# A hybrid decoder trunk on eight cores: a finer wrapping weight ring, squares and rotary sums on GpSimd, group-norm scaling on ScalarE

## The chip, the cores and the metric

The kernel runs on all 8 cores of one Trainium2 chip, one batch element per core, in one launch. Cores 0 to 3 are one die, 4 to 7 the other. The metric is the device time of the slowest core, in microseconds (us).

Every kernel of this program has a second, slower state: in some executions the cores of one die (sometimes both) are granted a lower TensorE clock and the run takes up to 20% longer. Such runs are called slow and no difference here rests on them. Where a kernel had hardly any fast run, I quote its **undisturbed dies**: the median span of the four cores of a die whose clock was not lowered.

## The reference, cut to what matters

Four layers over 2048 tokens of width 1024; per layer a half-weighted SwiGLU, a token mixer with two groups of heads, and a second SwiGLU.

```python
h = x + 1/2 * SwiGLU_1(RMSNorm(x))            # d_ff = 2816
u = RMSNorm(h); aq|ak|av|rq|rk|rv|rg = u @ W_in
a = sliding_window_gqa(aq, ak, av, sinks)     # window 128
r = retention(rotary(rq), rotary(rk), rv)     # chunks of 128, 4 heads of 128
r = silu(rg) * GroupNorm(r)
h = h + concat([a, r]) @ W_out
x = h + 1/2 * SwiGLU_2(RMSNorm(h))
```

## The kernel before

Each core takes its sequence as four tiles of 512 tokens, two at a time. The two tiles X = 0 and X = 1 go through each stage with the same weights. A host-side list scheduler, run when the kernel is built, fixes the order on each engine. Its priority is the TensorE time that comes earlier in the same tile, and tile 1 is set back by a constant, so that tile 0's next stage fills tile 1's waits.

```python
RING = 24576                     # columns of bf16 weights held on chip
LAG = 22.0
def key():
    X = cur['X']
    return cur['p'][X] + (LAG if X else 0.0)
```

The weights stream through one ring. A unit is 4096 columns of gate/up weights (32 matmuls of 512 columns for each tile), 2816 of w_down, or 4096 of w_o (half of the output projection). A unit that does not fit before the end of the ring starts again at zero, and its load waits for every use of every unit that it overlaps.

```python
for n, x in enumerate(units):
    size = x.size
    if head + size > RING:
        head = 0                         # the rest of the ring stays empty
    gone = [y for y in live if y.off < b and a < y.off + y.size]
    ...
    for y in gone:
        o.war |= {q.i for q, _ in y.uses}    # all uses of the whole unit
```

The sum of squares of a norm is built while the stage before it writes its eight chunks: ScalarE squares a chunk, and TensorE adds it across partitions with a matrix of ones.

```python
def np_feed(k):
    q = VT('b')
    act(AF.Square, lambda: T(q)[:], lambda: hT[X][:, k, :], ...)
    mm(lambda e: e.matmul(T(v)[:], onesd[:], T(q)[:], start=(i == 0), stop=(i == KC - 1)), ...)
```

In the mixer VectorE does the rotary products and sums, and the end of the group norm with the gate:

```python
for i in range(2):                       # rotary: two products, then two sums of halves
    dve(... tensor_tensor(out=q[.. i ..], in0=rt[i, first half], in1=rt[i, second half], op=ALU.add))
...
for h in range(4):                       # (y - mean) * rstd, per head
    dve(... tensor_scalar(out=T(yn)[:, hs], in0=T(vy)[:, hs], scalar1=mean, scalar2=rstd,
                          op0=ALU.subtract, op1=ALU.mult))
dve(... tensor_tensor(out=T(ro)[:], in0=T(yn)[:], in1=gsl(blk), op=ALU.mult))
```

The softmax here doesn't subtract the row's maximum and nothing guards it: scores larger than these inputs give would overflow.

## Time and profile before

| before | |
|---|---|
| all first runs, median (range) | 5324.35 us (5024.16 to 5688.27) |
| fast runs of all rounds | 5022 to 5036 us, with one of 5052 |
| profiled run, per core | 5001.8 to 5023.3 us, clock 0.989 to 0.991 |
| TensorE busy, idle | 4829.3, 194.0 us |
| VectorE, ScalarE, GpSimd busy | 37, 28, 6% |
| DMA packets | 64,543 for 362.92 MB |

The median of the first three runs mixes the two states; the fast runs have a mean of some 5,028 us.

In the profile, `L573` is line 573; PE, DVE, ACT and POOL are TensorE, VectorE, ScalarE and GpSimd; an entry after `<-` in brackets is what ended an idle stretch. TensorE's list of waits: line waited on, what released it, then us in all, times, and the longest. L539 is the ones-matmul of a norm, L573 the gate/up projection.

```profile
PE ps L539 <- ACT b L468: 36.2, 17, 7.1
PE ps L573 <- DVE nT L550: 29.1, 14, 4.7
PE ps L573 <- DMA ring<-w_gu: 9.8, 7, 2.5
```

The direct wait for weights is short. The two lines above it are the latency chain of a norm: square, ones-matmul, scale.

Second, GpSimd's timeline before one mixer's end (start, duration, then what ended the wait before it). These are the loads of the next gate/up units:

```profile
956.90 0.53 POOL L905 DMA_DIRECT2D ring<-w_gu  x1 [1.00 <-PE ps L609]
978.63 0.59 POOL L905 DMA_DIRECT2D ring<-w_gu  x1 [14.42 <-PE ps L609]
986.80 0.53 POOL L905 DMA_DIRECT2D ring<-w_gu  x1 [7.57 <-PE ps L740]
```

Three units, then none until the pair at 1057.68 that the prediction quotes. I quoted that pair, and did not count the three. The 42.90 us in its line are also not the whole pause: they count from GpSimd's last small copy (1014.10), while no load was issued for 70.9 us, from 986.80 on. At the eight seams, the places where a mixer hands over to the next gate/up stage, this pause was 51 to 71 us, always after three units.

One small VectorE operation with two on-chip inputs (duration min/median/max in ns):

```profile
L715 DVE TENSOR_TENSOR st<-st,epst x64: 145/155/275, 304.5 to 4750.6; 128x4 f32<-128x4 f32 x64
```

### The profile page before, as it was taken

The page shows a single profiled execution, that of the slowest core. Times are in us where ns is not written, and L with a number is a line of the kernel's source. Part 1 is how long each engine was busy: PE and PEld are TensorE (multiplying, and loading weights), DVE is VectorE, ACT ScalarE, POOL GpSimd, SP SyncE. Part 2 cuts the span into 40 slices and gives each one's busy share as a digit, 9 for nine tenths or more (in the row PEclk, how much of TensorE's full clock was granted, in tenths as well). Part 3 has the DMA queues.
Part 4 walks back from the last instruction along what each step waited for, and adds up shares of the span by engine and source line. Part 5 has one row for each costly group of instructions (what it writes and reads, how often), then busy time and mean ns, then how long its engine had stood idle before and what let it go on. Part 6 is the DMA issues. An engine that isn't in the chain of part 4 may idle for free.

```text
span 5023.3 us, 66149 instructions; the slowest of 8 cores (5001.8 to 5023.3 us)
## 1 busy us (share of the span) xinstructions
PE 4829.3 (96%) x23328; PEld 2235.8 (45%) x23800; DVE 1837.4 (37%) x3760; ACT 1413.1 (28%) x2346; POOL 277.2 (6%) x507
## 2 busy tenths in 40 slices
PE   8999999989999999999989999999999999999999
PEld 3444444434444444444434444444444444444444
DVE  2174122741227312173121741228322282222822
ACT  2144121441214412144121441214311153111521
POOL 1000000000000000000000000000000000000000
PEclk9999999999999999999999999999999999999999
DMA  6433344333443234433454333433334333344233
GB/s 128 77 67 54 71 75 78 64 52 71 75 79 65 52 71 78 78 65 65 72 127 71 71 66 71 79 72 64 63 68 82 68 62 68 72 74 75 54 73 74
DMA packets 64543, 362.92 MB, mean 72 GB/s; under 512 B 7904, under 2 KB 8160, under 8 KB 34656
## 3 DMA queue, kind: packets, MB, share of 16 engines
q0 software_dynamic: 53424, 339.76, 38.0%
q1 hardware_dynamic: 10800, 18.90, 1.3%
q8 instruction: 201, 3.29, 0.3%
q14 instruction: 118, 0.97, 0.1%
HBM read 689.98 MB, written 8.39 MB: 139 GB/s over the span
## 4 chain that ended last, share of the span: by engine, by line
PE 89%; ACT 3%; issue 3%; DVE 2%; DMA 2%; SPq 0%; DVEq 0%; POOL 0%; ACTq 0%; POOLq 0%
PE ps L573 46%; PE ps L584 24%; PE ps L609 8%; PE ps L830 4%; PE ps L740 2%; PE ps L539 2%; DMA ring<-w_gu 1%; ACT f L468 1%; ACT L468 1%; PE ps L647 1%; ACT b L468 1%; DMA hT<-xT 1%; PE ps L746 1%; PE ps L754 1%; PE ps L805 0%
## 5 line engine op out<-in xcount | busy, mean ns | idle before, releaser
L573 PE MATMUL ps<-nT,ring 128*128 128x512 bf16 x11027 | 2795.9, 382 | 58.7 <-DVE nT L550 29.1
L573 PEld LDWEIGHTS ps<-nT,ring 128*128 128x128 bf16 x11264 | 1105.6, 98 | 1397.8 <-issue 97.1
L584 PE MATMUL ps<-reg,ring 128*128 128x512 bf16 x5531 | 1651.4, 380 | 6.4
L577 DVE TENSOR_TENSOR reg<-ps,f 128x512 bf16<-128x512 f32 x704 | 477.5, 690 | 1954.9 <-PE ps L573 1777.3
L468 ACT ACTIVATE f<-ps 128x512 f32<-128x512 f32 (+1 forms) x884 | 515.9, 595 | 1927.7 <-PE ps L573 1867.7
L584 PEld LDWEIGHTS ps<-reg,ring 128*128 128x128 bf16 x5632 | 551.5, 98 | 661.6 <-issue 3.3
L609 PE MATMUL ps<-ring,nT 128*128 128x512 bf16 x1992 | 596.0, 379 | 10.2 <-ACT reg L468 2.7
L468 ACT ACTIVATE b<-hT 128x512 bf16<-128x512 f32 x416 | 258.6, 628 | 1031.3 <-DVE hT L586 868.3
L586 DVE SCALAR_TENSOR_TENSOR hT<-ps,hT 128x512 f32<-128x512 f32 x256 | 175.7, 690 | 805.3 <-PE ps L584 782.3
L468 ACT ACT_TABLE_LOAD x173 | 222.0, 1283 | 260.1 <-PE ps L573 139.4
L609 PEld LDWEIGHTS ps<-ring,nT 128*128 128x128 bf16 x2048 | 195.3, 98 | 218.4 <-issue 20.5
L550 DVE SCALAR_TENSOR_TENSOR nT<-hT,cn,f 128x512 bf16<-128x512 f32 x384 | 262.6, 748 | 60.5 <-ACT f L468 57.5
L830 PE MATMUL ps<-reg,ring 128*128 128x512 bf16 x996 | 251.8, 385 | 11.4 <-DVE reg L812 9.9
L905 POOL DMA_DIRECT2D ring<-w_gu x179 | 95.8, 536 | 2321.9 <-PE ps L573 1277.3
L468 ACT ACTIVATE b<-ps 128x512 bf16<-128x512 f32 (+1 forms) x312 | 175.6, 601 | 76.6 <-PE ps L647 59.4
L634 DVE TENSOR_TENSOR rt<-ps,rot 128x512 f32<-128x512 f32 x256 | 174.6, 682 | 61.1 <-PE ps L609 55.5
L539 PE MATMUL ps<-b,onesd 128*128 128x512 bf16 x402 | 154.4, 385 | 36.8 <-ACT b L468 36.2
L468 ACT ACTIVATE reg<-ps 128x512 f32<-128x512 f32 (+2 forms) x192 | 110.6, 598 | 200.5 <-PE ps L647 118.8
L830 PEld LDWEIGHTS ps<-reg,ring 128*128 128x128 bf16 x1024 | 99.0, 99 | 122.8 <-issue 19.9
L740 PE MATMUL ps<-nT,ring 128*128 128x512 bf16 x490 | 141.9, 379 | 2.2 <-DVE reg L728 0.9
L905 POOL DMA_DIRECT2D ring<-w_d x128 | 67.5, 530 | 1265.4 <-PE ps L573 1167.7
L832 DVE TENSOR_TENSOR hT<-ps,hT 128x512 f32<-128x512 f32 x128 | 87.1, 683 | 86.3 <-PE ps L830 83.4
(75 smaller groups left out, 1879.7 us busy)
## 6 DMA issues: line engine op xcount, KB each, us to landing
ring<-w_gu POOLq DMA_DIRECT2D x175, 1024.0 KB, 8.4
ring<-w_d POOLq DMA_DIRECT2D x128, 704.0 KB, 6.8
ring<-w_r POOLq DMA_DIRECT2D x32, 1024.0 KB, 8.9
ring<-w_o POOLq DMA_DIRECT2D x16, 1024.0 KB, 8.1
hT<-xT SPq DMA_DIRECT2D x32, 256.0 KB, 7.4
ring<-w_aq POOLq DMA_DIRECT2D x8, 1024.0 KB, 8.8
yT<-reg SPq DMA_DIRECT2D x32, 256.0 KB, 4.8
ring<-w_akv POOLq DMA_DIRECT2D x8, 512.0 KB, 5.1
```

The costliest lines, as they stand in the source:

```text
L468: return A('act', lambda e: e.activation(out=out(), in_=in_(), func=func, **{k: (v() if callable(v) else v) for k, v in kw.items()}), read ...
L539: mm(lambda e: e.matmul(T(v)[:], onesd[:], T(q)[:], start=(i == 0), stop=(i == KC - 1)), [q, 'onesd'], [v])
L550: dve(lambda e, k=k: e.scalar_tensor_tensor(out=dst(k), in0=hT[X][:, k, :], scalar=cn[:, cbase + k:cbase + k + 1], in1=T(r)[:], op0=ALU.mu ...
L573: mm(lambda e, v=v, a=a, k=k, x=x: e.matmul(T(v)[:], W(x, a, 128), nT[X][:, k, :], start=(k == 0), stop=(k == KC - 1)), [('n', X, k)], [v] ...
L577: dve(lambda e, sg=sg, pu=pu, fc=fc: e.tensor_tensor(out=reg[X][:, fc, :], in0=T(pu)[:], in1=T(sg)[:], op=ALU.mult), [pu, sg], rk(X, fc))
L584: mm(lambda e, v=v, fc=fc, x=x: e.matmul(T(v)[:], W(x, fc * 128, 128), reg[X][:, fc, :], start=(fc == 0), stop=(fc == FC - 1)), rk(X, fc), ...
L586: dve(lambda e, v=v, dc=dc: e.scalar_tensor_tensor(out=hT[X][:, dc, :], in0=T(v)[:], scalar=0.5, in1=hT[X][:, dc, :], op0=ALU.mult, op1=AL ...
L609: mm(lambda e, k=k: e.matmul(T(v)[:], nT[X][:, k, blk * 128:(blk + 1) * 128], W(x, k * 512, 512), start=(k == 0), stop=(k == KC - 1)), [(' ...
L634: dve(lambda e, i=i, off=off: e.tensor_tensor(out=rt[:, i, :].rearrange("p (h e) -> p h e", h=4), in0=X4(), in1=rot[:, g + off:g + off + 1 ...
L740: mm(lambda e, k=k, j=j, v=v: e.matmul(T(v)[:], W(xa, (k * 4 + j) * 128, 128), nT[X][:, k, :], start=(k == 0), stop=(k == KC - 1)), [('n', ...
L830: mm(lambda e, v=v, a=a, src=src, x=x, cc=cc: e.matmul(T(v)[:], W(x, a, 128), R_[:, src, :], start=(cc == 0), stop=(cc == 7)), rk(X, src), ...
L905: o = rec.add('pool', lambda e, x=x, j=j, w=w: e.dma_start(out=ring_t[:, x.off + j * w:x.off + (j + 1) * w], in_=x.src[:, j * w:(j + 1) * w]),
```

## The change

The intent is to take work from TensorE (squares) and from VectorE (rotary sums, group norm), to lay both on nearly idle engines, and to let weights arrive earlier. The core of the diff; `...` marks cuts. Two edits are not shown: 16 semaphores instead of 12 for the weight loads, and GpSimd operations that now wait for the one before.

```diff
-LAG = 22.0
+LAG = 23.0
+RESERVE = {'ps': 0, 'f': 1, 'b': 2, 'st': 1}     # buffers the scheduler keeps back
...
-            if eng == 'pool':
-                writes = list(writes) + ['poolq']      # GpSimd in program order
...
+            x.step = 2048 if x.size % 2048 == 0 else x.size // 2
...
-        def np_start():
+        def np_start(direct=False):
...
+            if acc is not None and i == 0:
+                act(AF.Square, lambda: T(acc)[:], lambda: hT[X][:, k, :], [('h', X, k)], [acc])
+                return
+            if acc is not None and i < KC - 2:
+                out = acc if i < KC - 3 else VT('b')
+                A('pool', lambda e: e.tensor_tensor(out=T(out)[:], in0=T(acc)[:], in1=T(q)[:], op=ALU.add), ...)
...
-                for i in range(2):
-                    dve(... tensor_tensor(... op=ALU.add), [('rt', i)], [q], 0.42)
+                A('pool', lambda e: e.tensor_tensor(out=T(q)[:]..., in0=half(0), in1=half(1), op=ALU.add), ...)
...
-                    dve(... tensor_scalar(... op0=ALU.subtract, op1=ALU.mult), [vy, st], [yn], 0.3)
+                    act(AF.Identity, T(yn)[:, hs], T(vy)[:, hs], ..., scale=rstd, bias=-mean*rstd)
-                dve(... tensor_tensor(out=T(ro)[:], in0=T(yn)[:], in1=gsl(blk), op=ALU.mult), ...)
+                A('pool', ... same operation ...)
...
-            if head + size > RING:
-                head = 0
+                q.a, q.b = a, min(a + x.step - a % x.step, a + RING - head)
+                head = (head + w) % RING
...
+                while live and live[0].off < q.off + w and q.off < live[0].off + live[0].b - live[0].a:
+                    o.war |= {z.i for z in live.popleft().uses}
```

## The prediction

> **What bounds the kernel now.** I read the cores first: 5001.8 to 5023.3 us, both dies alike, clock 0.99, a fast run. (The quoted median, 5324 us, mixes states; the lowest, 5024 us, is the fast one. I predict the fast state and compare with 5023.) The engine totals:
>
> ```profile
> PE 4829.3 (96%) x23328; PEld 2235.8 (45%) x23800; DVE 1837.4 (37%) x3760; ACT 1413.1 (28%) x2346; POOL 277.2 (6%) x507
> ```
>
> TensorE looks full, but matmul records overlap, so I count work. The chain of waits in order of time and the timeline of TensorE give its two rates:
>
> ```profile
> 93.86 10.74 PE ps L573 x49
> ...
> 1006.36 1.06 PE L754 MATMUL ps<-ring,nT 128*128 128x128 bf16 x16
> ```
>
> One 512-column matmul lasts 0.38 us, so 49 in 10.74 us is (10.74-0.38)/48 = 0.2158 us each; the 128-column ones take (1.06-0.22)/15 = 0.056. The code issues 21,528 of the first kind (1,344 for each of 16 tile-layers, 32 for the first norms, less 8 for the first block) and 2,272 of the second: 4,646 + 127 = **4,773 us** that no schedule removes. The other 250 us are 194 us of recorded idle time and about 55 us of lost clock (mean 0.989, 1.1% of the span). By windows of 25 us, the idle time lies at the start (21), the end (13), the turn to the second pair of tiles (17 at 2500-2550), six ends of FFN stages (21), and the eight mixer stages (103); 20 us are scattered. Here is a mixer, with busy time and count of PE, PEld, DVE, ACT, POOL, then clock, DMA share, GB/s:
>
> ```profile
> 925.00:950.00 25.00, 23.25 (x158) 12.39 (x160) 22.52 (x77) 9.86 (x20) 1.05 (x2) 1.00 0.46 85
> 950.00:975.00 25.00, 20.85 (x142) 10.81 (x144) 23.45 (x61) 18.39 (x35) 5.08 (x9) 1.00 0.25 43
> 975.00:1000.00 25.00, 24.84 (x158) 13.01 (x160) 22.77 (x68) 10.75 (x22) 1.12 (x2) 1.00 0.48 86
> 1000.00:1025.00 25.00, 19.97 (x121) 9.65 (x121) 19.92 (x47) 17.01 (x32) 5.15 (x8) 1.00 0.01 1
> 1025.00:1050.00 25.00, 20.02 (x84) 8.31 (x86) 12.09 (x23) 22.55 (x29) 0.00 (x0) 0.97 0.00 1
> 1050.00:1075.00 25.00, 22.11 (x90) 9.46 (x91) 10.72 (x16) 9.43 (x13) 1.65 (x3) 0.90 0.61 93
> ```
>
> Three limits follow one another: VectorE is at 90% or more for 75 us; then ScalarE is at 90% while no weights move at all; then TensorE waits at the seam. The timeline shows why the DMA stood still (Pool first, then TensorE):
>
> ```profile
> 1057.68 1.13 POOL L905 DMA_DIRECT2D ring<-w_gu  x2 [42.90 <-PE ps L830]
> ```
> ```profile
> 1066.57 0.38 PE L539 MATMUL ps<-b,onesd 128*128 128x512 bf16 x1 [1.51 <-ACT b L468]
> 1068.06 2.89 PE L573 MATMUL ps<-nT,ring 128*128 128x512 bf16 x8 [1.12 <-DMA ring<-w_gu]
> ```
>
> The next gate/up unit could not be issued until the second tile had finished with a whole w_o unit, 42.90 us later; then TensorE had only the norm's chain to wait for (1.51 us) and then the weights (1.12).
>
> **What the Trainium skill says.** "ScalarE: Activation LUTs", What ACT_TABLE_LOAD costs: 186 ns + 0.833 ns per column, 93 ns more for each pointer operand, 93 ns overlap; 512 columns make 613 ns, and the trace has 596 to 628, so it agrees. The same page, Table sets, says identity is in every set: no new table load. "GPSIMD Engine Reference", 3.1: a two-input tensor_tensor runs at about 2.6 cycles per element, 4497 ns at 2048 columns; nothing in the trace checks that, as Pool does none. "SBUF — State Buffer", Who interferes with whom: a VectorE instruction with two SBUF inputs and a GpSimd instruction that reads SBUF exclude each other for the whole instruction. The trace fits: the same small Pool copy takes 288 ns mostly and once 1373.
>
> ```profile
> L819 POOL COPY kprev<-kd x24: 282/288/1373, 335.3 to 4704.6; 64x127 bf16<-64x127 bf16 x24
> ```
>
> **The change, part by part.** The rows it touches:
>
> ```profile
> L539 PE MATMUL ps<-b,onesd 128*128 128x512 bf16 x402 | 154.4, 385 | 36.8 <-ACT b L468 36.2
> ```
> ```profile
> L638 DVE TENSOR_TENSOR b<-rt 128x256 bf16<-128x256 f32 x256 | 107.4, 419 | 5.1 <-DVE b L638 0.5
> L722 DVE TENSOR_SCALAR f<-ps,st 128x128 f32<-128x128 f32 x256 | 103.4, 405 | 5.4 <-ACT st L468 3.7 <-DVE st L712 0.3
> L726 DVE TENSOR_TENSOR b<-f,reg 128x512 bf16<-128x512 f32 x64 | 43.6, 682 | 0.1
> ```
>
> *Squares.* For 48 norms (16 tile-layers x 3; the first norm of each tile stays) six of the eight squares are added on GpSimd and three ones-matmuls remain: 48 x 5 = 240 matmuls less, 240 x 0.2158 = **52 us** of TensorE time. These sit among full streams, so nearly all should show: I book 50. The last two squares still go straight to TensorE, so the end of a norm is no longer. The price is 240 Pool adds, by the skill's slope 1.1 us and some 0.2 of dispatch each (an estimate): 1.3 us against one output chunk per 1.73 us in w_o and 4.7 us in w_down. It keeps up.
>
> *Ring.* Units of 4096 and 2816 columns become parts of 2048 and 1408 that wrap anywhere. Before w_o, 2048 columns were skipped; now all are used, and a slot is freed by half a unit. In the seam above the next half unit can go out after two chunks of w_o instead of four (3.9 us earlier) and lands sooner (a 512 KB load took 5.1 us, a 1 MB one 8.4). Six FFN ends (21 us) and eight seams like that of 1066 (2.6 us each) make 42 us; I book 25. The cost is about 780 issues instead of 371 at 0.53 us on Pool.
>
> *VectorE relief.* 107.4 + 103.4 + 43.6 less 64 new small operations at 0.157 = 244 us off VectorE, 30 per mixer. Its 90% stretches fall to some 65%. Idle TensorE time in those first three windows is about 5 us per mixer, 40 in all; I book 22. The price: 256 Identity operations on ScalarE, 186 + 2 x 93 + 0.833 x 128 - 93 = 386 ns each (estimate), 99 us or 12 per mixer, and Pool hops. The rotary buffer is single, so a rotation becomes 2 x 0.68 on VectorE + 1.3 on Pool + two handovers, some 3 us instead of 2.2, with one projection per 1.73 us of TensorE time shared by two tiles. I book -8 for the busier ScalarE late in the mixer and the longer hops.
>
> *Clock.* Fewer idle stretches, fewer dips: 10 of the 55 us. In all 50 + 25 + 22 - 8 + 10 = 99, and a few from the scattered 20 us and from a lag of 23 instead of 22: about **118 us**, 5023 to **4905 us** (-2.3%).
>
> Pool afterwards: 240 + 128 + 64 = 432 operations x 1.3 = 562, plus 413 for issues and about 75 as now: 1,050 us, 21%. It does not become the bound on average.
>
> **Rivals.** *ScalarE becomes the bound of the mixer.* For it: 22.55 of 25 us already, and the new work goes there. Against: the group norm comes before the attention, in windows where ScalarE has 10 to 18 of 25. It would eat the VectorE gain and more: about 4,945. *Pool in order.* Weight issues and adds now share one queue; an issue that waits up to 64.6 us for a slot (the longest in the list of waits) holds up an add behind it, and a two-input VectorE operation can hold up both. Against: the order is fixed by a schedule that knows these waits, and Pool is 94% idle. It would cost some us per stage, 4,930 to 5,000. *Everything fits.* If both TensorE stretches in the mixers fill up, idle time falls to 80 and the time to 4,773 - 52 + 80 + 40 = 4,841. *The loads were hidden anyway.* Direct waits for weights are only 9.8 us in the list; if the norm chain behind them stays, 4,920.
>
> **Range and chances.** The 50 us are nearly certain, the rest uncertain by some 50: 4,845 to 4,980. The 2% line is 4,923, so faster by over 2% 0.6, within 2% 0.38, slower 0.02.
>
> **What would show it.** Ones-matmuls from 416 to 176; VectorE at about 1,590 us; ScalarE at about 1,510; Pool near 1,050 with its two-input operations at 1.2 to 1.5 us; recorded TensorE idle time from 194 to about 135; DMA no longer at zero for 40 us in a mixer; no waits of TensorE on Pool over 1 us. I am wrong if those operations take 2 us or more under contention, if TensorE waits on Pool or ScalarE for over 60 us in the mixers, or if the seams stay as long.

## The result, and the profile after

The results are correct. Four runs of the changed kernel gave 4879 to 5497 us, median 4882.4; the fast ones lie between 4879 and 4884. The kernel before, on the same chip, had a median of 5179.84 of four runs. A ratio here is the mean time of one kernel's fast runs over that of the other's of the same rounds, so not quite the ratio of the medians. It is **0.9705**, with a 95% interval of 0.9677 to 0.9733: about 148 us, or 2.95%, faster. The profiled run was fast, 4871.2 to 4877.5 us on its cores at clock 0.995 to 0.996.

The engine totals after:

```profile
PE 4774.9 (98%) x23560; PEld 2205.1 (45%) x23560; DVE 1714.0 (35%) x3248; ACT 1544.1 (32%) x2620; POOL 1000.2 (21%) x1310
```

The same mixer, by windows of 25 us (columns as in the prediction: busy time and count of PE, PEld, DVE, ACT, POOL, then clock, DMA share, GB/s):

```profile
925.00:950.00 25.00, 21.73 (x142) 11.12 (x140) 16.06 (x34) 16.40 (x34) 14.23 (x17) 0.93 0.29 52
950.00:975.00 25.00, 22.66 (x166) 12.44 (x164) 22.83 (x71) 16.82 (x36) 9.81 (x9) 1.00 0.25 43
975.00:1000.00 25.00, 23.66 (x139) 11.15 (x137) 15.78 (x34) 17.94 (x37) 13.14 (x16) 1.00 0.41 65
1000.00:1025.00 25.00, 23.34 (x104) 9.72 (x103) 14.72 (x29) 24.03 (x34) 0.00 (x0) 1.00 0.00 1
1025.00:1050.00 25.00, 25.00 (x118) 11.29 (x117) 12.59 (x19) 10.04 (x14) 7.94 (x9) 1.00 0.52 85
```

In the first half of the mixer TensorE still idles 3.27 us in one window although VectorE has only 16 of 25 us; in the next, VectorE is at 22.83 again. In the second half ScalarE is fuller than ever (24.03) and no weights move, as before, and yet TensorE has 23.34 us and then all 25. Before, these two windows had 19.97 and 20.02 (the changed kernel reaches its seam some 26 us earlier, so the same times are not quite the same work). TensorE's timeline says what fills them (start, duration, line, operation, count):

```profile
1013.08 11.60 PE L618 MATMUL ps<-nT,ring 128*128 128x512 bf16 x53
1024.51 13.98 PE L874 MATMUL ps<-reg,ring 128*128 128x512 bf16 x64
1038.33 1.03 PE L618 MATMUL ps<-nT,ring 128*128 128x512 bf16 x4
...
1041.13 19.16 PE L618 MATMUL ps<-nT,ring 128*128 128x512 bf16 x88
```

L618 is the gate/up projection of tile 0, one stage ahead; L874 is tile 1's output projection. Gate/up work runs right up to the projection and is still there after it, so the chain of tile 1's norm is covered. GpSimd's timeline shows the weights for it: eight half units were issued from 920.48 to 988.56 (the last two are the first lines here). No load was then issued for 40.2 us, 29.61 of them with GpSimd idle, and it no longer mattered.

```profile
983.41 0.59 POOL L941 DMA_DIRECT2D ring<-w_gu  x1
988.56 0.59 POOL L941 DMA_DIRECT2D ring<-w_gu  x1 [0.54 <-PE ps L829]
1028.73 0.59 POOL L941 DMA_DIRECT2D ring<-w_gu  x1 [29.61 <-PE ps L874]
1032.62 0.57 POOL L941 DMA_DIRECT2D ring<-w_gu  x1
```

TensorE's waits after (L585 is now the ones-matmul, L690 the turn of a rotated block):

```profile
PE ps L585 <- ACT b L495: 20.5, 10, 6.3
PE ps L690 <- POOL b L683: 8.3, 7, 1.9
PE ps L618 <- DVE nT L595: 5.2, 7, 3.8
```

The wait of gate/up for the scaled norm fell from 29.1 to 5.2 us although that operation was not touched. Before the change, VectorE had itself idled for 57.5 us before this operation, waiting for ScalarE's part of the norm; so no backlog of VectorE shows there. The groups of the moved work (busy us, mean ns of one, then idle time of its engine before):

```profile
L577 POOL TENSOR_TENSOR f<-f,b 128x512 f32<-128x512 f32 x192 | 221.9, 1156 | 482.8 <-ACT b L495 473.6
L683 POOL TENSOR_TENSOR b<-rt 128x512 bf16<-128x512 f32 x128 | 163.4, 1277 | 227.6 <-DVE rt L679 134.9
L495 ACT ACTIVATE f<-ps,st 128x128 f32<-128x128 f32 x256 | 116.4, 459 | 35.0 <-DVE st L763 23.5 <-DVE st L757 3.2 <-DVE st L758 0.7
```

And the small VectorE operation again, whose median is nearly as before, but not its longest:

```profile
L758 DVE TENSOR_TENSOR st<-st,epst x64: 145/163/1459, 305.1 to 4607.4; 128x4 f32<-128x4 f32 x64
```

**Where the 146 us of the two profiled runs went** (5023.3 to 4877.5).

- *Work.* 240 ones-matmuls less make 240 x 0.2158 = 52 us.
- *Idle time.* Recorded idle time fell from 194.0 to 102.6 us, but the two numbers are not alike. The trace before lacks 472 matmul records (23,328 of the 23,800 whose weight loads it has), the trace after none. In a full stream a missing record leaves a hole of 2 x 0.2158 - 0.38 = 0.05 us, 24 us in all (an estimate). So the true figure before is about 170. Core 2 of the same execution, as long to within 0.2 us (5023.1) and with every record, has 164.6. Idle time fell by some 62 to 67 us.
- *Rate.* The sum over all 25-us windows of busy time times (1 - clock) is 44 us before and 17 after; 22 windows were below clock 0.97 before, 8 are after. That is 27 us.

52 + 67 + 27 = 146. That this fits exactly is chance: with core 2 in place of the estimate it is 52 + 62 + 28 = 142 (its sum of the rate is 45). By windows, and with the holes still in the first numbers, idle time went from 103 to 52 in the eight mixers, from 21 to under 2 at the FFN ends, from 17 to 8.5 at the turn to the second pair of tiles, and stayed at the start (21 to 22) and the end (13 to 10).

### The profile page after: what moved, and what is told of

It is laid out like the page before. It is cut to its first block, busy times and chain, and to the rows that moved or that the text cites.

```text
span 4877.5 us, 69117 instructions; the slowest of 8 cores (4871.2 to 4877.5 us)
## 1 busy us (share of the span) xinstructions
PE 4774.9 (98%) x23560; PEld 2205.1 (45%) x23560; DVE 1714.0 (35%) x3248; ACT 1544.1 (32%) x2620; POOL 1000.2 (21%) x1310
## 4 chain that ended last, share of the span: by engine, by line
PE 92%; issue 2%; ACT 2%; DVE 2%; DMA 1%; POOL 1%; DVEq 0%; SPq 0%; ACTq 0%; POOLq 0%
PE ps L618 49%; PE ps L629 25%; PE ps L654 8%; PE ps L874 4%; PE ps L784 2%; ACT f L495 1%; DMA ring<-w_gu 1%; PE ps L690 1%; PE ps L585 1%; PE ps L849 1%; ACT b L495 1%; PE ps L829 1%; DMA hT<-xT 1%; PE ps L790 0%; POOL b L683 0%
## 5 line engine op out<-in xcount | busy, mean ns | idle before, releaser
L618 PE MATMUL ps<-nT,ring 128*128 128x512 bf16 x11264 | 2845.0, 379 | 18.7 <-DMA ring<-w_gu 7.7
L618 PEld LDWEIGHTS ps<-nT,ring 128*128 128x128 bf16 x11264 | 1099.8, 98 | 1353.7 <-issue 48.1
L629 PE MATMUL ps<-reg,ring 128*128 128x512 bf16 x5632 | 1700.7, 380 | 0.0
L654 PE MATMUL ps<-ring,nT 128*128 128x512 bf16 x2048 | 623.9, 381 | 2.8 <-ACT reg L495 1.2
L941 POOL DMA_DIRECT2D ring<-w_gu x354 | 193.5, 548 | 1714.0 <-PE ps L618 1111.4
L495 ACT ACTIVATE b<-hT 128x512 bf16<-128x512 f32 x368 | 229.9, 630 | 912.4 <-DVE hT L631 816.7
L941 POOL DMA_DIRECT2D ring<-w_d x268 | 143.4, 537 | 920.0 <-PE ps L618 894.5
L577 POOL TENSOR_TENSOR f<-f,b 128x512 f32<-128x512 f32 x192 | 221.9, 1156 | 482.8 <-ACT b L495 473.6
L595 DVE SCALAR_TENSOR_TENSOR nT<-hT,cn,f 128x512 bf16<-128x512 f32 x384 | 274.2, 779 | 72.8 <-ACT f L495 68.4
L874 PE MATMUL ps<-reg,ring 128*128 128x512 bf16 x1024 | 252.4, 379 | 0.0
L683 POOL TENSOR_TENSOR b<-rt 128x512 bf16<-128x512 f32 x128 | 163.4, 1277 | 227.6 <-DVE rt L679 134.9
L784 PE MATMUL ps<-nT,ring 128*128 128x512 bf16 x512 | 164.8, 379 | 1.3 <-ACT st L495 0.8
L874 PEld LDWEIGHTS ps<-reg,ring 128*128 128x128 bf16 x1024 | 98.1, 98 | 105.7
```

The costliest lines, as they stand in the source:

```text
L495: return A('act', lambda e: e.activation(out=out(), in_=in_(), func=func, **{k: (v() if callable(v) else v) for k, v in kw.items()}), read ...
L577: A('pool', lambda e: e.tensor_tensor(out=T(out)[:], in0=T(acc)[:], in1=T(q)[:], op=ALU.add), [acc, q], [out], 1.3)
L595: dve(lambda e, k=k: e.scalar_tensor_tensor(out=dst(k), in0=hT[X][:, k, :], scalar=cn[:, cbase + k:cbase + k + 1], in1=T(r)[:], op0=ALU.mu ...
L618: mm(lambda e, v=v, a=a, k=k, x=x: e.matmul(T(v)[:], W(x, a, 128), nT[X][:, k, :], start=(k == 0), stop=(k == KC - 1)), [('n', X, k)], [v] ...
L629: mm(lambda e, v=v, fc=fc, x=x: e.matmul(T(v)[:], W(x, fc * 128, 128), reg[X][:, fc, :], start=(fc == 0), stop=(fc == FC - 1)), rk(X, fc), ...
L654: mm(lambda e, k=k: e.matmul(T(v)[:], nT[X][:, k, blk * 128:(blk + 1) * 128], W(x, k * 512, 512), start=(k == 0), stop=(k == KC - 1)), [(' ...
```

## The experiments

**Theory, the gate.** What counts is how much gate/up work of tile 0 is on chip when tile 1's attention and output projection begin, because the next load after that waits for a w_o slot. **Rivals.** The VectorE relief unlocked TensorE; the squares alone explain most of it; or side edits (lag, reserve, free order on GpSimd) do.

### All combinations of the three parts

Each part was undone by a short edit of the changed kernel; its bookkeeping (lag 23, reserve, free GpSimd order, and the two edits not shown) stayed.

```diff
# squares undone
-        def np_start(direct=False):
+        def np_start(direct=True):
# ring undone
-            x.step = 2048 if x.size % 2048 == 0 else x.size // 2
+            x.step = x.size
+            if head + x.size > RING: head = 0
-                q.a, q.b = a, min(a + x.step - a % x.step, a + RING - head)
+                q.a, q.b = a, a + x.step
-                while live and live[0].off < q.off + w and ...:
+                while any(y.off < q.off + w and q.off < y.off + y.b - y.a for y in live):
# relief undone: rotary sums, group norm's scaling and gating as in the kernel before
-                A('pool', ... op=ALU.add ...)   /  act(AF.Identity ...)  /  A('pool', ... op=ALU.mult ...)
+                dve(... op=ALU.add ...) x 2     /  dve(tensor_scalar ...) /  dve(... op=ALU.mult ...)
```

Expected of everything but the squares (ring and relief):

> All of the change but the squares: all eight squares of every norm go through a ones-matmul again (416 of them instead of 176). Theory: TensorE's own work decides, 240 x 0.2158 us = 52 us come back, so 4,930 us (ratio to before about 0.982). Rival: part of them fell into time in which TensorE was idle anyway, then 10 to 35 us come back (4,890 to 4,915 us); or the Pool adds also shortened something, then over 60.

Of everything but the ring (squares and relief):

> All of the change but the fine ring: whole units of 4096 and 2816 columns again, no unit wraps, a unit's slot is freed as a whole. Theory: the seams behind w_o and the ends of the FFN stages get their idle time back, 35 to 50 us, so 4,915 to 4,930 us; ones-matmuls stay 176. Rival (the loads were hidden, the schedule filled the seams otherwise): under 15 us, 4,880 to 4,895 us.

Of everything but the relief (ring and squares):

> All of the change but the moves within the mixer: rotary sums, gating and group norm scaling are on VectorE again. Theory: VectorE is the limit of the first 75 us of a mixer again, 40 to 55 us come back, 4,920 to 4,935 us, VectorE near 1,850 us busy. Rival (my prediction's booking of this part): 14 us net, 4,895 us. Rival (ScalarE and Pool hops cost as much as they give): no change or faster than 4,880.

> The third run once more, as it had only slow executions: the change without the moves within the mixer. Theory: VectorE at 90% in the first part of the mixers costs 40 to 55 us, 4,920 to 4,935 us. Rival, my booking of 14 us net: 4,895 us.

Of none of the three:

> All three parts undone; what stays is the schedule's bookkeeping (lag 23 for 22, buffers kept in reserve, Pool's operations no longer tied to the order of the program). Theory: these do nothing by themselves, 5,010 to 5,030 us, ratio 0.998 to 1.002. Rival: the schedule's settings are a good part of the gain: 4,970 to 5,000 us.

Of the ring alone, the squares alone, and the relief alone:

> The fine ring alone; squares, rotary sums, gating and scaling as before. After the second run (without the ring the two other parts bring nothing, 5,007 us like the run with all three undone) the theory is a gate: with whole units the first tile runs out of weights until the second tile's output projection frees a slot, and what is saved elsewhere only lengthens the wait there. Then the ring alone should bring a part of it by itself, 40 to 70 us: 4,940 to 4,970 us. Rival: the ring is worth its 125 us in every setting, 4,885 us. Rival: the parts only work together, 4,990 us or more.

> The squares on GpSimd alone, with whole units in the ring. Gate theory: 52 us of TensorE's work are gone and the time falls by less than 25 us against the run with all three undone (over 4,985 us), the idle time of TensorE grows instead. Rival (TensorE's work bounds, parts add): 52 us less, 4,950 to 4,960 us.

> Rotary sums, gating and scaling moved alone, with whole units and all squares on TensorE. Gate theory: within 25 us of the run with all three undone, 4,985 to 5,025 us. Rival (VectorE bounded the mixers, parts add): 40 us less, 4,965 us.

Measured (the dies are the range of the undisturbed dies' medians):

| kernel | fast runs, us | ratio to before, 95% | undisturbed dies, us |
|---|---|---|---|
| before | 5022 to 5036, 5052 | 1 | 5005 to 5016 (5019 to 5022 at clock 0.987) |
| none | 5004 to 5010 | 0.9957 (0.9928 to 0.9986) | 4990 to 4999 |
| relief | 5016, 5017 | 0.9976 (0.9952 to 1.0000) | 4997 to 5001 |
| squares | 4986, 4992, 5020 | 0.9955 (0.9905 to 1.0005) | 4970 to 4978 |
| squares, relief | 5004 to 5009 | 0.9957 (0.9935 to 0.9980) | 4983 to 4993 |
| ring | 4946, 4947, 4982 | 0.9861 (0.9809 to 0.9913) | 4938 to 4943 |
| ring, relief | 4948 to 4955 | 0.9846 (0.9826 to 0.9865) | 4936 to 4948 |
| ring, squares | 4886 to 4887 | 0.9718 (0.9699 to 0.9737) | 4878 to 4889 |
| all three | 4879 to 4884 | 0.9705 (0.9677 to 0.9733) | 4874 to 4880 |

Each part's worth depends on the ring. In fast runs the **ring** takes 61 us off alone (5007 to 4946, leaving out the run of 4982, in which one die was at 0.989), 66 where the relief is there (5016 to 4950), about 103 where the squares are there (4989 to 4886), and 125 where squares and relief are (5006 to 4881). The **squares** take 60 us off with the ring (4946 to 4886), 69 with ring and relief (4950 to 4881), and 18 without (5007 to 4989, leaving out the run of 5020, in which one die was at 0.987; by the ratios, which keep it, nothing, within 25 us). The **relief** takes about 5 us off with ring and squares, nothing with the ring alone, and costs 9 to 18 without the ring, all within the intervals. The bookkeeping takes 21. The kernels ran on different chips, and each edit makes the scheduler order everything anew, so differences of 10 to 20 us may be no more than that.

Several expectations missed: without the ring 4,915 to 4,930 us were expected and 5,006 came; without the relief 4,920 to 4,935 and 4,886; without the squares 4,930 and 4,950. The first miss led to the theory of the gate.

Why do the squares give so little without the ring? The engine totals of "none" and then of "squares":

```profile
PE 4821.7 (96%) x23328; PEld 2235.6 (45%) x23800; DVE 1836.9 (37%) x3760; ACT 1411.8 (28%) x2340; POOL 280.2 (6%) x507
```
```profile
PE 4776.6 (96%) x23094; PEld 2211.8 (44%) x23560; DVE 1849.1 (37%) x3760; ACT 1410.7 (28%) x2338; POOL 561.3 (11%) x747
```

Of spans of 5008.1 and 4984.7 us, TensorE is idle 186.4 and 208.1 us (both traces lack some 470 records, so the difference is fair). Of 45 us of busy time saved, 22 came back as idle time. The six cores of each profile that have every record agree: busy time 46 us less, idle time 25 more (means 145 to 170). With ring and relief in place, the squares lower busy time by 61 and idle time by 6. The ring lowers the mean idle time of such cores from 145 to 109 us alone, and from 175 to 103 where squares and relief are.

With squares and relief but the old ring, GpSimd's timeline has three gate/up units again, the last at 997.76, and then

```profile
997.76 0.59 POOL L943 DMA_DIRECT2D ring<-w_gu  x1 [1.71 <-PE ps L690]
1045.49 1.15 POOL L943 DMA_DIRECT2D ring<-w_gu  x2
```

and TensorE's timeline at this seam is

```profile
1024.75 9.44 PE L618 MATMUL ps<-nT,ring 128*128 128x512 bf16 x43
...
1037.38 14.07 PE L874 MATMUL ps<-reg,ring 128*128 128x512 bf16 x64 [2.75 <-DVE reg L856]
...
1053.46 0.42 PE L585 MATMUL ps<-b,onesd 128*128 128x512 bf16 x1 [1.49 <-ACT b L495]
1055.56 19.80 PE L618 MATMUL ps<-nT,ring 128*128 128x512 bf16 x91 [1.67 <-DMA ring<-w_gu]
```

Gate/up work runs out before tile 1's attention is done; TensorE waits for its tail (2.75 us), then, after the projection, for the norm's square (1.49) and for weights (1.67). In the changed kernel none of these waits exists at the same place. The relief was in this kernel: with VectorE at 34% of the span the seam still waits. The other way round, with the ring and the squares but without the relief, two windows in the first half of the mixer read

```profile
900.00:925.00 25.00, 24.92 (x152) 12.26 (x150) 23.09 (x71) 10.38 (x20) 2.11 (x4) 1.00 0.48 82
925.00:950.00 25.00, 20.85 (x146) 10.64 (x144) 23.85 (x60) 14.22 (x29) 5.28 (x10) 1.00 0.26 47
```

VectorE is back above 23 of 25 us, and the kernel is as fast to within 5 us. Between 900 and 1050 TensorE has 139.5 us of busy time here and 141.4 with the relief, while VectorE has 114.1 and 103.9. VectorE was full there and did not set the time: from 900 to 1000 TensorE is busy for 93.1 us in both (93.4 in the kernel before), with VectorE at 91.7 and 76.6.

### How far ahead: wrap, parts, and ring length

The code says how many units are ahead. In the old ring the w_o units lie so that at each of the eight seams the fourth gate/up unit overlaps the first w_o unit (and the key/value unit before it): I followed the allocation for all eight, and it is always three units. Without the skipped columns the lead is RING less the 8192 columns of w_o: 16,384 columns, four units. Four experiments vary it on the changed kernel: whole units that wrap (four units, freed late); half units that do not wrap (three and a half by the trace: seven halves are issued before the stop); and the fine ring shortened by 2048 (three and a half) and 4096 columns (three).

```diff
# wrap only
-            x.step = 2048 if x.size % 2048 == 0 else x.size // 2
+            x.step = x.size
# parts only
+            if head + x.size > RING: head = 0        # and parts kept whole
# shorter rings
-RING = 24576
+RING = 22528      # and 20480
```

> All of the change, but the ring in whole units that may only be cut where the ring ends (4096 and 2816 columns, no skipped columns). It splits the ring's 126 us into its two properties. Theory (capacity: the skipped columns held the first tile back): 60 us or more of the 126 us are kept, 4,940 us or less. Rival (freeing by half units did it): near the run without the ring, 4,985 to 5,007 us.

> All of the change, but a unit that doesn't fit at the end of the ring starts at its beginning again; loads and freeing go by half units. Theory (early freeing is the larger part): 4,890 to 4,930 us. Rival (the used capacity is what counts): 4,960 us or more.

> The whole change with the ring 2,048 columns shorter (22,528 for 24,576). Gate theory: half a unit less of lead for the first tile at each of 16 stage turns, 2 to 4 us each, so 30 to 60 us slower than the change: 4,910 to 4,940 us. Rival (the lead is not what bounds): within 10 us of 4,881.

> The whole change with a fine ring of 20,480 columns (five units instead of six): the first tile now gets 3 gate/up units ahead of the second tile's output projection, as in the kernel before, but the next half unit can still go out after two chunks. Theory (the lead in weights is the gate; 4 units: 4,881, 3.5 units: 4,900 and 4,892): 4,930 to 4,990 us, with TensorE waiting for the attention before the output projection and for weights behind it at each mixer. Rival (only early freeing counts): under 4,920 us.

Measured:

| lead at the seam | fast runs, us | undisturbed dies, us |
|---|---|---|
| 3 units, coarse (squares, relief) | 5004 to 5009 | 4983 to 4993 |
| 3 units, fine, 20480 columns | 4954 (5007, 5008 with one die at 0.985) | 4945 to 4948 |
| 3.5 units, parts only | 4938 (one die at 0.986) | 4890 to 4893 |
| 3.5 units, fine, 22528 columns | 4901 | 4894 to 4897 |
| 4 units, wrap only, freed late | 4911.5 | 4902 to 4905 |
| 4 units, fine | 4879 to 4884 | 4874 to 4880 |

These kernels were slow most of the time, so no ratio is to be had; the undisturbed dies agree within a few us for each kernel. Lead and early release both count: at three units the fine ring is some 40 us faster, though it is 4096 columns shorter, and at four units the halves are worth some 27 (they are released earlier and also land sooner; the two are not separated). The ring of 22528 columns was expected at 4,910 to 4,940 us and came out better. Three and a half units give nearly the same time in two quite different rings, which speaks for the lead itself. The shortest ring shows its wait at the expected line: its list of waits has

```profile
PE ps L874 <- DVE reg L856: 31.7, 9, 4.5
```

the wait of the output projection for tile 1's attention, 31.7 us against 29.3 with the coarse ring; in the changed kernel no wait of this line is listed at all. The kept traces show the same of the others: with a lead of three units this wait is 9.9 us before, 7.6 in "none", 3.2 with the relief and 15.5 with the squares; with three and a half fine units it is 5.7; in every kernel with four units (ring alone, with relief, with squares, wrap only, lag 22) it is 0.4 us or none.

From three fine units to four the time falls by 72 us, 9 per seam. A unit holds 32 x 0.2158 = 6.9 us of work, so 55 us for eight seams (an estimate). On the cores with every record, idle time is 46 us longer with three units (148.9 against 102.6) and busy time 28 us, for the same matmuls: by the sum over windows 38 us are lost to a lower clock, against 17.

### The bookkeeping: lag, reserve, order on GpSimd

"None" is 21 us faster than before without any of the three parts. Three of its side edits were undone one at a time, and the lag also in the changed kernel; the two edits not shown above were never undone.

```diff
# lag (on "none", and on the changed kernel)
-LAG = 23.0
+LAG = 22.0
# order (on "none")
+            if eng == 'pool':
+                writes = list(writes) + ['poolq']
# reserve (on "none")
-RESERVE = {'ps': 0, 'f': 1, 'b': 2, 'st': 1}
+RESERVE = {'ps': 0, 'f': 0, 'b': 0, 'st': 0}
```

> All three parts undone, and Pool's operations tied to the order of the program again; lag 23 and the reserve of buffers stay. It asks what made the run with all three parts undone 22 us faster than the kernel before. If it was the freed order on Pool: 5,022 to 5,030 us. If not: 5,004 to 5,010 us.

> All three parts undone, and no buffers kept in reserve; lag 23 and the freed order on Pool stay. If the reserve made the 22 us: 5,022 to 5,030 us. If neither this nor the order on Pool does: both 5,004 to 5,010 us, and the lag or chance in the schedule remains.

> All three parts undone and the old lag of 22; the reserve of buffers and the freed order on Pool stay. If the lag made the 22 us by which the run with all three parts undone beats the kernel before: 5,022 to 5,030 us. If not: 5,004 to 5,012 us, and the order on Pool (5,017 us in its one undisturbed run) is the likelier cause.

> The whole change with the old lag of 22 us between the tiles. Theory: the lag matters little, within 10 us of the change (4,875 to 4,892 us). Rival: the 22 us that the bookkeeping alone brought (5,007 against 5,029) came from the lag, then 4,895 us or more.

- Lag 22 in "none": 5030.8 to 5038.3 us, ratio 1.0001 (0.9968 to 1.0034). The whole 21 us are gone with this one edit.
- Lag 22 in the changed kernel: 4879.5 and 4879.8 us, ratio 0.9714 (0.9686 to 0.9743). Nothing changes. With four units ahead this step of the lag makes no difference.
- Reserve: six slow runs; undisturbed dies 4996 to 5002 against 4990 to 4999. No effect that these runs could show.
- Order: one fast run, 5017.4 us, others slow, undisturbed dies 5004 to 5022 against 4990 to 4999. The dies point to a loss of 10 to 20 us here too. Two edits that each take most of 21 us away do not add up; the gain belongs to one schedule rather than to the lag alone.

Where do the lag's 21 us sit? On the six cores of each profile that have every record, the mean idle time is 158.5 us with lag 22 and 145.2 with 23, and the mean busy time, for the same matmuls, 4858.2 and 4843.9. On the slowest cores the sum of busy time times (1 - clock) is 52 and 34 us. So about half is less waiting and half fewer clock dips. Why one us of lag does that I did not settle.

### Scaling on ScalarE, and one more square on GpSimd

The prediction set 8 us against the relief for a busier ScalarE. One run puts only the group norm's scaling back on VectorE; another tries to go further, with seven squares on GpSimd and two ones-matmuls.

```diff
# scaling back on VectorE
-                    act(AF.Identity, ..., scale=rstd, bias=-mean*rstd)
+                    dve(... tensor_scalar(... op0=ALU.subtract, op1=ALU.mult))
# two ones-matmuls
-            if acc is not None and i < KC - 2:
-                out = acc if i < KC - 3 else VT('b')
+            if acc is not None and i < KC - 1:
+                out = acc if i < KC - 2 else VT('b')
```

> The change without the group norm's scaling on ScalarE (it is on VectorE again; rotary sums and gating stay on GpSimd). It asks why the moves within the mixer bring only some 5 us. If the busier ScalarE (24 of 25 us late in the mixers) eats a gain of the two Pool moves: 4,865 to 4,875 us. If VectorE was never on the path: within 5 us of the change, 4,876 to 4,886 us. If the scaling was the part that helped: 4,887 us or more.

> A version meant to beat both: the change with seven of the eight squares added on GpSimd and two ones-matmuls per norm instead of three (48 fewer, 48 x 0.2158 = 10 us). Theory: 4,868 to 4,874 us, if the sixth addition does not lengthen the end of a norm; rival: the added Pool step sits on the path at the seams, 4,880 to 4,895 us.

Scaling on VectorE: 4885.3 to 4886.0 us, ratio 0.9704 (0.9634 to 0.9775), and dies at 4878 to 4883 against 4874 to 4880: some 4 us slower than the changed kernel, about what the whole relief seems worth, and as little clear of the noise. No sign that ScalarE's new work eats a gain.

Two ones-matmuls: 4879.8 and 4881.1 us, no gain, although 48 matmuls or 10 us of work are gone. Its TensorE is busy for 4774.1 us, against 4774.9, and its wait for the scaled norm rose to 10.4 us from 5.2. But its idle time in all is 104.1 us against 102.6, so the saving was not lost in waiting. It was lost in the rate: the sum of busy time times (1 - clock) is 26 us against 17, at a mean clock of 0.994 against 0.996. Whether the kernel or its chip (not the same one) lowers the clock is open. It is a tie with the changed kernel.

## Why the prediction was right or wrong

**The time and the reference state.** 4,905 us was 23 above what was measured, inside the range. The comparison must be fast with fast: 5,023 to 4,905 is 118 us or 2.3%, measured 148 us or 2.95%. Set against the quoted median of 5,324, a mix of states, the same 4,905 reads as a gain of 419 us, or 7.9%, and no pair of like runs shows that. The direction was right; the gain was forecast a fifth too small. That the total came so near is partly luck: the ring was booked far too low, and the relief and the scattered idle time too high.

**Squares, "I book 50".** The ones-matmuls fell to 176, and 60 to 69 us showed, with the ring in place (52 of work, the rest mostly rate). The reason given, "These sit among full streams, so nearly all should show", was true of the changed kernel only. Without the ring 18 us show and 22 to 25 come back as idle time. The term was right and its condition was missing.

**Ring, "I book 25": the step that failed most.** It measured 61 us alone and 66 to 125 with other parts. The text noted "Before w_o, 2048 columns were skipped; now all are used" and gave that no price. What it priced was the gate opening 3.9 us earlier and shorter landings, that is, what happens after the gate has closed. The skipped columns are what makes three units ahead into four; that covers tile 1's tail and norm before the gate matters at all. With the lead cut back to three units the fine ring loses 72 us again. The other half of the term came true: the idle time at the six FFN ends, 21 us before and 19 without the ring, is under 2. The lines for it were there: three issues and then none for 51 to 71 us, at every seam. "I am wrong ... if the seams stay as long" looked the right way; the pauses are now 36 to 42 us, behind eight half units.

**VectorE relief, "I book 22" and "-8": wrong step.** "Three limits follow one another: VectorE is at 90% or more for 75 us" was read as a limit since the engine was full. All combinations together give some 5 us at most, and a cost without the ring. With VectorE at 23 of 25 us the time hardly moved. Nor did "90% stretches fall to some 65%" hold: one window is at 16 of 25 us, its neighbours at 21.95 and 22.83. And the room on VectorE did not become work of TensorE: in those windows, 925 to 975, it idles 5.6 us after and 5.9 before. The chain of waits had named gate/up waits for the norm and not VectorE's backlog. The busier ScalarE did not cost 8 either, although it was at 24.03 of 25 us in a window.

**Clock, "10 of the 55 us".** By the sum over windows it measured 27.

**Scattered idle time and lag, booked at about 19 in all ("a few").** Undoing the lag costs 21 us or more without the ring and nothing with it. The "20 us scattered" were largely holes of missing records (24 us by the estimate above, 29 by core 2), not time that a schedule could fill. In all, idle time was forecast to fall by 59 us and fell by 62 to 67.

**Rivals.** "The loads were hidden anyway" is false: how early loads may go is the largest single part. "ScalarE becomes the bound" and "Pool in order" did not come true: GpSimd's 1.15 to 1.28 us per operation fit the estimate of 1.3, and TensorE's wait on GpSimd is 8.3 us for the rotary sums and some 12 in all, far from the 60 us set as a sign of being wrong. It is longer at its longest (1.9 us) than the 1 us allowed. "Everything fits" (4,841) was too good: 52 us of idle time stay in the mixers.

**Sizes of the smaller forecasts.** VectorE 1,590 forecast, 1,714 measured; ScalarE 1,510 and 1,544; GpSimd 1,050 and 1,000; recorded idle time 135 and 103. "DMA no longer at zero for 40 us" failed, as one window still has 0.00 and one wait is 29.61 us; it was a poor test, because a pause behind a large enough lead is harmless. VectorE's shortfall has three visible parts. The forecast subtracted the lengths of the removed records, but records of VectorE overlap: their lengths sum to 2,027 us before and 1,838 after, its busy time to 1,837 and 1,714, so 65 us of what was taken away had been hidden under neighbours. Operations with two on-chip inputs stretched beside GpSimd (L758's longest from 275 to 1459 ns, the scaled norm's mean from 748 to 779 ns), as the Trainium skill, "SBUF — State Buffer", Who interferes with whom, says such pairs exclude each other. This trace agrees: all 20 of the 64 L758 operations that took over 1.3 times the median overlap a GpSimd operation in time, and 5 of the other 44. And the new 4-column operation took 421 ns on average instead of the 157 assumed, with a median of 161: it stretches too. ScalarE's excess is mostly table loads, 191 for 173, of 1.28 us each; the Identity does not force them, as the changed kernel with lag 22 has 169 and ScalarE at 1,510 us. ScalarE's Identity took 459 ns and not the 386 worked out from "ScalarE: Activation LUTs", What ACT_TABLE_LOAD costs; but 386 has the overlap with a neighbour taken off, and a single record compares with 479, as the prediction's own check at 512 columns (613) did.

## What to carry to other kernels

When two streams share weights in a ring, count at each seam how many units of the next stage can be on chip before the first load that must wait for a slot still in use, and compare their work with the longest latency chain of the other stream; that lead, not the sum of direct weight waits, tells what a finer ring is worth. A saving of work on the bound engine is only collected where that engine has something else ready, so price the two together; an engine at 90% beside the bound is no limit until a wait names it. Before counting idle time, check that the trace has all of the bound engine's records.

## What the Trainium skill lacked or had wrong

- "TensorE: Matmul & The Clock Gate", Part 1, tells to budget 13/16 of the clock for dense matmuls on three or more cores of a die. Here dies ran at a mean of 0.985 to 0.996 in fast runs; means of 0.81 to 0.98 appear only on dies in the slow state (0.76 and 0.78 in two outliers).
- The same page, Why this matters for your kernels, asks for no idle gaps over about 3 us between bursts. The runs agree in part: single gaps of 3 us or more number 9 before, 13 with squares and relief but the old ring, and 3 after; windows of 25 us below clock 0.97 number 22, 28 and 8. But the changed kernel has a window at clock 0.80 (325 to 350 us) with no gap over 1.8 us and 5.9 us of idle time in sum, and a window with 4.0 us of idle time at full clock. A single long gap is not needed.
- "Perfetto Trace Analysis", Identifying the Most-Contended Engine, warns that matmul busy time is a poor measure, and Optimization Strategy that regular bubbles can mean too few buffers; both fit (TensorE was 96% busy, and the ring still gave 61 to 125 us). It does not say that matmul records can be missing: 472 of 23,800 here, on two of the eight cores, worth about 24 us of false idle time (an estimate).
- "ScalarE: Activation LUTs", What ACT_TABLE_LOAD costs: its figures give 479 ns for one 128-column Identity with two pointer operands, and 386 with the overlap of back-to-back ones. The record lasts 459 ns on average, so the first is nearly met; but where one Identity follows another, the starts are mostly 553 ns apart, and only 9 of 85 pairs are under 380. The overlap did not show in most pairs here.
- No page that I read has the lag between two interleaved streams as a parameter: in the kernel with the coarse ring, one us less of it cost 21 us or more, and with the fine one nothing.
